# The FFN's normed rows turned on TensorE, three blocks' first products early, and the final norm's squares by halves, in an fp32 xLSTM/ConvFFN kernel

## The chip, the cores and the metric

The kernel runs on one core of a Trainium2 chip. The metric is the device time of one launch in microseconds. Three runs of the kernel before gave 1116.49, 1116.83 and 1116.87 us: a median of 1116.83. The trace is of one further execution of 1116.72 us, whose recorded span is 1115.0 us, so 1.72 us lie outside the span. Times below are us from the span's start.

The engines: TensorE (PE) multiplies, with its weight loads listed apart as PEld; VectorE (DVE) and ScalarE (ACT) work elementwise; GpSimd (POOL) does small things here; SyncE (SP) issues most DMAs. An engine's rows with a `q` at the end (SPq, ACTq) are its queue's own, such as DMA issues. Each engine runs its instructions strictly in its own order and waits on semaphores for the others.

## The reference

One layer on x of 1024 tokens x 1024, all fp32:

```python
x = x + mlstm_mixer(rmsnorm(x, norm_mix), ...)             # matrix memory in chunks of 64, then @ w_out
x = x + conv_ffn(rmsnorm(x, norm_ffn), w_up, conv_w, conv_b, w_down)
return rmsnorm(x, final_norm)

def rmsnorm(x, g):
    return x * lax.rsqrt(jnp.mean(x * x, axis=-1, keepdims=True) + EPS) * g
def conv_ffn(x, w_up, conv_w, conv_b, w_down):
    u = causal_dwconv(x @ w_up, conv_w, conv_b)            # 1024 -> 2 * 2816, width 3 along tokens
    gate, val = u[..., :2816], u[..., 2816:]
    return (jax.nn.silu(gate) * val) @ w_down              # 2816 -> 1024
```

The change touches what lies between the mixer's output projection and the up-projection, and the end.

## The kernel before

Every fp32 product is made of three matmuls in a rounded form (`mm3`, L119): each operand is split into a high part (`whi`, a cast on ScalarE) and the rest (`wlo`, a subtraction on VectorE), and low x high, high x high, high x low are summed in PSUM. "Matmul" below is one instruction with 128 x 128 weights and 512 columns.

Stages: norm and transposes of the input; projections; the mLSTM chunks up to about 345 us; the output projection by column halves, `out_proj(0, t)` and then `out_proj(1, t)` for the eight token tiles t (PSUM `pout`, added to the residual x on VectorE at L553); the FFN's norm; up-projection; down-projection; final norm.

**Seven products.** Up- and down-projection replace a 2 x 2 block product by seven block products (a Strassen-like scheme). For the up-projection tokens are halved (t < 4 and t >= 4) and the model dimension too. The seven right operands are b11, b21 (from the first tokens alone), b22 (second tokens alone), and the sums and differences t1 to t4 of quarters. Each is kept as a pair of high and low parts, `yc_...`; `put` (L615) writes one token tile of one of them: a cast of 128 x 512 on ScalarE (L620) and a subtraction on VectorE (L621). The rows of `yc_b...` are b11, b21, b22, those of `yc_t...` t1 to t4.

**Turning.** The operands need the normed rows `y` turned, with the model dimension on the partitions. `ffn_norm` (L623) takes the squares on ScalarE, the root on GpSimd (`rstd`), and makes both halves of y on VectorE (L628). For t < 7, y is written to DRAM block by block (`y_d`), read back as `flip_r`, and each half is turned within blocks of 32 by VectorE (`flip_halves`, L647, STREAM_TRANSPOSE at L652). For t = 7 eight TensorE transposes with an identity turn it in PSUM (`tp`, L659), and ScalarE copies both halves out (L660). `mix_a` (L662) then makes the differences and calls `put`.

**Up-projection.** 22 blocks of 128 hidden columns of gate and value, in the order 0, 11, 1, 12, 2, ... (HF = 11). A block needs its weights' pieces (`prep_first`: the gate's, `prep_rest`: value and sums, L703 to L727) and seven products of twelve matmuls, 84 in all, in `up` (L761). The results come together in `ug` and `uv` in SBUF: ScalarE copies a PSUM bank as a first term (L772, L775, L777, L787), VectorE adds others (L781, L783, L785). The products need six operands that are late, but b11 and b21 are complete early: `early` (L735) runs products 1 and 2 (`px`, `py`) of blocks 0 and 11 ahead of the turning of t = 7. Then come `pz`, the product with t1, and the others on the `px` and `pz` banks. PSUM has eight banks of 512 fp32 columns, here in groups: pa (two), pb (two), pc (four). `ug` and `uv` lie in the pool `late`, which is opened only after the pool `d2` with the turned rows is closed, so after the `put`s of t4 (L755 to L759).

**Down-projection.** Seven products again (924 matmuls, `pd`), the last of them, called 4, for the first column half: its blocks' weights come through the same `pieces` (L707, L708). It first finishes rows t = 0 to 3 beside it, then t = 4 to 7 at the very end. The final norm of row t: squares of both halves on ScalarE (L178, in `rms_scale`), root on GpSimd, the product of the first half with the gain (L896, GpSimd; VectorE for t = 7), its scaling on ScalarE (L902), the second half on VectorE (L904); the first half's output DMA is issued by ScalarE, the second's by SyncE (L903, L907), where the weight loads of the last blocks also queue.

The order of the instructions on each engine is set by a scheduler when the kernel is built, from the program's dependencies and the pools' buffers; `after` (L93) adds an order by hand in some places.

Of the kernel before, what the change touches and what calls it, by code (L numbers as in the profile page):

```python
# [43 lines left out]
def xlstm_convffn(  # L44
# [591 lines left out]
    def halves(t):  # L636
        lo_k = d2.tile([P, 516], F32, name="f0", tag="d2")[:, :512]
        if t < 4:
            if t % 2 == 0:
                b21[t // 2] = a4.tile([P, 2, 512], F32, name="b21", tag="a4")  # L640
            hi_k = b21[t // 2][:, t % 2]
        else:
            hi_k = d2.tile([P, 516], F32, name="f1", tag="d2")[:, :512]
        half_t[t] = [lo_k, hi_k]
        return half_t[t]
# [8 lines left out]
    def turn_halves(t, y):
        for a, dst in enumerate(halves(t)):
            ps = psa.tile([P, 512], F32, name="tp", tag="pc", bufs=4)
            yv = y[:, a * 512:(a + 1) * 512].rearrange("t (p k) -> t k p", k=4)
            for i in range(4):
                nc.tensor.transpose(ps[:, i * P:(i + 1) * P], yv[:, i], ident)  # L659
            nc.scalar.copy(dst, ps)  # L660

    def mix_a(t):  # L662
        f = half_t[t]
        if t < 4:
            if t == 0:
                combo("b11")
                combo("b21")
            put("b11", t, f[0])
            put("b21", t, f[1])
            return  # L670
# [24 lines left out]
    def prep_load(j):  # L695
        rg, rv = [rawp.tile([P, 1056], F32, name="raw", tag="raw") for _ in range(2)]
        for r, m in ((rg, j), (rv, NF + j)):
            v = r[:, :1024].rearrange("p (k c) -> p k c", c=P)
            for a in range(2):
                nc.sync.dma_start(out=v[:, a * NQ:(a + 1) * NQ], in_=w_up_v[:, a, :, m * P:(m + 1) * P])  # L700
        return rg[:, :1024], rv[:, :1024]
# [9 lines left out]
    def prep_first(j):  # L711
        rg, rv = prep_load(j)
        a11, a12 = pieces(rg)
        return rg, rv, a11, a12

    def prep_rest(rg, rv, a11, a12):
# [263 lines left out]
```

## Time and profile before

| what | value |
|---|---|
| median of three runs | 1116.83 us (1116.49 to 1116.87) |
| the profiled execution, its span | 1116.72 us, 1115.0 us |
| TensorE busy | 1071.9 us, 96% |
| VectorE, ScalarE, GpSimd busy | 775.5, 481.9, 77.4 us (70%, 43%, 7%) |
| TensorE's share of the chain that ended last | 77%; VectorE 11% |
| granted TensorE clock, mean over the span | 0.987 |
| bytes moved by DMA | 144.97 MB, 130 GB/s |
| last `pout` matmul, first `px`, first `pd`, last `pd` (starts) | 424.63, 424.87, 881.92, 1104.22 us |

The busy shares are of the whole span. The record of a busy matmul overlaps the next one, so a matmul's price is read from start to start. [...]

### The profile page before, as it was taken

Reading aid. Unit: us, or ns where it says so; the run is one execution under the profiler, and the core shown is the slowest. Engines: PE = TensorE matmul, PEld = TensorE weight load, DVE = VectorE, ACT = ScalarE, POOL = GpSimd, SP = SyncE. Lnnn points to the kernel's source line nnn. Section 1 sums busy time; section 2 is a strip of 40 time slices with the busy share of each in tenths; the row PEclk is TensorE's granted clock in tenths of the full one; section 3 lists DMA queues with packets and bytes.
Section 4 is the critical chain, followed back from the end, with each engine's and each line's share of the span. In section 5 each row is a group of like instructions: output and inputs, shape, how many; then the busy total and the mean of one; then the engine's idle time right before and its main releaser. Section 6 shows DMA issues by size and latency. Waiting matters only on the chain.

```text
span 1115.0 us, 13445 instructions
## 1 busy us (share of the span) xinstructions
PE 1071.9 (96%) x4918; PEld 876.6 (79%) x4918; DVE 775.5 (70%) x1146; ACT 481.9 (43%) x722; POOL 77.4 (7%) x155
## 2 busy tenths in 40 slices
PE   8999999999999995799999999999999999999985
PEld 7988888888887884588888888888888888888874
DVE  6733211488788469998978788787878778556564
ACT  6233111365453234454545454454545534433354
POOL 2000000123220011000000000000000000000042
PEclk9999999999999998799999999999999999999998
DMA  7722311024228475213331332233132895345653
GB/s 255 222 76 71 91 43 57 29 81 128 61 92 288 152 233 163 76 57 123 115 125 44 123 123 82 98 110 127 48 123 95 309 305 166 98 134 188 188 189 113
DMA packets 126091, 144.97 MB, mean 130 GB/s; under 512 B 8407, under 2 KB 87239, under 8 KB 126024
## 3 DMA queue, kind: packets, MB, share of 16 engines
q1 hardware_dynamic: 124872, 142.01, 39.5%
q10 hardware_dynamic: 1152, 2.10, 0.5%
q8 instruction: 38, 0.62, 0.2%
q14 instruction: 29, 0.24, 0.1%
HBM read 105.51 MB, written 38.57 MB: 129 GB/s over the span
## 4 chain that ended last, share of the span: by engine, by line
PE 77%; DVE 11%; DMA 4%; ACT 3%; issue 3%; POOL 2%; SPq 0%; POOLq 0%; ACTq 0%; DVEq 0%
PE px L122 7%; PE px L121 7%; PE px L120 7%; PE pd L121 5%; PE pd L120 5%; PE pd L122 5%; PE pz L122 4%; PE pz L121 4%; PE pz L120 3%; PE pqk L122 3%; PE pqk L121 3%; PE pqk L120 3%; PE pv L120 2%; PE pv L122 2%; PE pv L121 2%
## 5 line engine op out<-in xcount | busy, mean ns | idle before, releaser
L120 PE MATMUL pd<-wlo,whi 128*128 128x512 f32 x308 | 122.9, 399 | 4.2 <-DVE wlo L708 4.2
L707 ACT CAST whi<-raw 128x1024 fp32r<-128x1024 f32 x77 | 80.7, 1049 | 105.1 <-PE py L121 37.2
L121 PE MATMUL pd<-whi 128*128 128x512 f32 x308 | 122.9, 399 | 0.0
L122 PE MATMUL pd<-whi,wlo 128*128 128x512 f32 x308 | 121.1, 393 | 0.0
L120 PE MATMUL px<-yc_t,whi 128*128 128x512 f32 x264 | 105.2, 399 | 5.7 <-ACT ug L772 5.5
L708 DVE TENSOR_TENSOR wlo<-raw,whi 128x1024 fp32r<-128x1024 f32 x77 | 94.4, 1230 | 23.3 <-ACT whi L707 23.1
L122 PE MATMUL px<-yc_t,wlo 128*128 128x512 f32 x264 | 105.6, 400 | 0.0
L121 PE MATMUL px<-yc_t,whi 128*128 128x512 f32 x264 | 105.4, 399 | 0.0
L116 DVE TENSOR_TENSOR wlo<-raw,whi 128x1024 fp32r<-128x1024 f32 (+1 forms) x30 | 37.1, 1238 | 55.4 <-ACT whi L114 55.1
L120 PEld LDWEIGHTS pd<-wlo,whi 128*128 128x128 f32 x308 | 58.3, 189 | 20.9 <-DVE wlo L708 6.0
L707 ACT CAST whi<-s 128x1024 fp32r<-128x1024 f32 (+1 forms) x44 | 36.8, 836 | 77.2 <-PE px L121 39.4
L122 PEld LDWEIGHTS pd<-whi,wlo 128*128 128x128 f32 x308 | 58.1, 189 | 14.6
L114 ACT CAST whi<-raw 128x1024 fp32r<-128x1024 f32 (+1 forms) x30 | 31.3, 1051 | 87.1 <-PE pqk L121 37.4
L121 PEld LDWEIGHTS pd<-whi 128*128 128x128 f32 x308 | 58.1, 189 | 12.8
L120 PEld LDWEIGHTS px<-yc_t,whi 128*128 128x128 f32 x264 | 50.5, 191 | 18.7 <-ACT ug L772 5.9
L121 PEld LDWEIGHTS px<-yc_t,whi 128*128 128x128 f32 x264 | 50.2, 190 | 12.3
L122 PEld LDWEIGHTS px<-yc_t,wlo 128*128 128x128 f32 x264 | 50.2, 190 | 11.7
L796 DVE SCALAR_TENSOR_TENSOR acc<-ug,cw,acc 128x1024 f32<-128x1024 f32 x44 | 56.2, 1278 | 1.4 <-ACT acc L794 1.3
L796 DVE SCALAR_TENSOR_TENSOR acc<-uv,cw,acc 128x1024 f32<-128x1024 f32 x44 | 56.2, 1278 | 0.1
L881 ACT CAST whi<-raw 128x512 fp32r<-128x512 f32 x44 | 27.3, 621 | 59.4 <-PE pd L122 40.7
L882 DVE TENSOR_TENSOR wlo<-raw,whi 128x512 fp32r<-128x512 f32 x44 | 30.2, 687 | 27.7 <-ACT whi L881 27.6
L708 DVE TENSOR_TENSOR wlo<-s,whi 128x1024 fp32r<-128x1024 f32 (+1 forms) x44 | 41.9, 955 | 3.1 <-ACT whi L707 3.0
(265 smaller groups left out, 2680.6 us busy)
## 6 DMA issues: line engine op xcount, KB each, us to landing
raw<-in_l_ffn_w_up_dram SPq DMA_DIRECT2D x88, 256.0 KB, 3.4
raw<-h_d SPq DMA_DIRECT2D x77, 256.0 KB, 2.8
h_d<-acc SPq DMA_DIRECT2D x22, 512.0 KB, 3.4
raw<-in_l_ffn_w_down_dram SPq DMA_DIRECT2D x44, 256.0 KB, 3.5
h_d<-hx SPq DMA_DIRECT2D x11, 768.0 KB, 3.9
raw<-in_l_mlstm_w_in_dram SPq DMA_DIRECT2D x14, 512.0 KB, 5.0
keep<-in_l_ffn_w_down_dram SPq DMA_DIRECT2D x22, 256.0 KB, 4.6
raw<-in_l_mlstm_w_in_dram SPq DMA_DIRECT2D x16, 256.0 KB, 3.7
```

The source lines that it names most:

```text
L114: nc.scalar.copy(hi[:, :n], raw[:, :n])
L116: nc.vector.tensor_sub(lo[:, :n], raw[:, :n], hi[:, :n].bitcast(F32))
L120: nc.tensor.matmul(ps, a[0], b[1], start=first, stop=False, skip_group_check=chain)
L121: nc.tensor.matmul(ps, a[0], b[0], start=False, stop=False, skip_group_check=chain)
L122: return nc.tensor.matmul(ps, a[1], b[0], start=False, stop=last, skip_group_check=chain)
L707: nc.scalar.copy(hi[:, :n], src)
L708: nc.vector.tensor_sub(lo[:, :n], src, hi[:, :n].bitcast(F32))
L796: nc.vector.scalar_tensor_tensor(out=acc, in0=u[:, 2 - d:1026 - d], scalar=cw[:, tap, m:m + 1], in1=acc, op0=ALU.mult, op1=ALU.add)
L881: nc.scalar.copy(hi[:, sl], v)
L882: nc.vector.tensor_sub(lo[:, sl], v, hi[:, sl].bitcast(F32))
```

## The change

1. The row tiles t = 4, 5, 6 are turned like t = 7: by TensorE, with eight transposes each (`turned`). VectorE's differences and `put` read `tp` in PSUM directly; ScalarE copies one half of each row. `y_d` and `flip_halves` are left for t < 4. The pool for the read-backs has two buffers instead of three.
2. Three blocks' first products run early: 0, 11 and 1; block 1's in bank group pc. The gate's weights of these are loaded and split first; `prep_rest` loads the gate's weights again (512 KB more for each of the three).
3. `ug` of blocks below 11 has a pool of its own (`ugp`), opened earlier; `hx` goes from pool `sp` to `late`.
4. The final norm's square of a half is taken right after that half's last addition, by halves; the product with the gain is taken of the half that does not come last (GpSimd), and all output DMAs but the very last are issued by ScalarE.

```diff
-    flip_cm = tc.tile_pool(name="flip", side="right", bufs=3, reuse_waits="tile")
+    ugp_cm = tc.tile_pool(name="ugp", side="right", bufs=1, reuse_waits="tile")
+    flip_cm = tc.tile_pool(name="flip", side="right", bufs=2, reuse_waits="tile")
...
-            if t < NT - 1:
+            if t < 4:
                 flip_out(n, y[:, sl], y_d[t][:, :])
...
+    def turned(y, a, last):
+        ps = psa.tile([P, 512], F32, name="tp", tag="pa" if last else "pc", bufs=2 if last else 4)
+        yv = y[:, a * 512:(a + 1) * 512].rearrange("t (p k) -> t k p", k=4)
+        for i in range(4):
+            nc.tensor.transpose(ps[:, i * P:(i + 1) * P], yv[:, i], ident)
+        return ps
 
     def turn_halves(t, y):
         if t == 4:
             combo("b22")
             combo("t1")
+        b12, b22 = [turned(y, a, t == NT - 1) for a in range(2)]
         g = half_t[t - 4]
-        nc.vector.tensor_sub(g[0], f[0], g[0])
+        f = d2.tile([P, 516], F32, name="f0", tag="d2")[:, :512]
+        half_t[t] = [f]
+        nc.vector.tensor_sub(g[0], b12, g[0])
+        nc.scalar.copy(f, b12)
         put("t1", t, g[0])
-        nc.vector.tensor_sub(g[0], f[1], g[0])
-        nc.vector.tensor_sub(f[0], f[1], f[0])
+        put("b22", t, b22)
+        nc.vector.tensor_sub(g[0], b22, g[0])
+        nc.vector.tensor_sub(f, b22, f)
         nc.vector.tensor_sub(g[1], g[1], g[0])
-        put("b22", t, f[1])
...
-        if t >= 2:
+        if 2 <= t < 6:
             flip_halves(t - 2)
-            mix_a(t - 2)
-    flip_halves(NT - 2)
-    mix_a(NT - 2)
+        elif t >= 6:
+            turn_halves(t - 2, ys[t - 2])
+    turn_halves(NT - 2, ys[NT - 2])
...
-    for j in (0, HF):
-        first[j] = prep_first(j)
-    bank = {j: early(first[j]) for j in first}
-
+    for j, tag, bufs in ((0, "pb", 2), (HF, "pb", 2), (1, "pc", 4)):
+        first[j] = pieces(prep_load(j))
+        bank[j] = early(first[j], tag, bufs)
     turn_halves(NT - 1, ys[NT - 1])
-    mix_a(NT - 1)
-    ready = {0: prep_rest(*first[0])}
+    ready = {0: prep_rest(0, first.pop(0))}
...
-        ug = late.tile([P, 1028], F32, name="ug", tag="ug", bufs=2)
+        ug = (late if j >= HF else ugp).tile([P, 1028], F32, name="ug")
...
-        hx = sp.tile([P, 3, 512], F32, name="hx")
+        hx = late.tile([P, 3, 512], F32, name="hx")
...
+    def final_sq(t, n):
+        junk = const.tile([P, 512], BF16, name="junk", tag="junk")
+        nc.scalar.activation(junk, x1v(t, n), AF.Square, scale=1.0 / 32.0, accum_out=fss[:, t, n:n + 1])
+
+    def final_a(t):
         y = a4.tile([P, D], F32, name="yo", tag="a4")
-        eng = nc.vector if t == NT - 1 else nc.gpsimd
-        eng.tensor_tensor(y[:, :512], xv[0], g_fin[:, :512], op=ALU.mult)
-        fin[t] = (y, rms_scale(xv, "rstdf"))
+        n = 1 if t >= 4 else 0
+        nc.gpsimd.tensor_tensor(y[:, n * 512:(n + 1) * 512], x1v(t, n), g_fin[:, n * 512:(n + 1) * 512], op=ALU.mult)
+        r = small.tile([P, 1], F32, name="rstdf")
+        nc.gpsimd.tensor_scalar(
+            out=r, in0=fss[:, t, 0:1], scalar1=fss[:, t, 1:2], scalar2=EPS, op0=ALU.add, op1=ALU.add
+        )
+        nc.gpsimd.tensor_tensor(r, r, mhalf[:, :1], op=ALU.pow)
+        fin[t] = (y, r)
 
     def final_b(t):
...
-        nc.scalar.activation(y[:, :512], y[:, :512], AF.Copy, scale=r)
-        nc.scalar.dma_start(out=o[:, :512], in_=y[:, :512])
+        n = 1 if t >= 4 else 0
+        a, b = slice(n * 512, n * 512 + 512), slice((1 - n) * 512, (1 - n) * 512 + 512)
+        nc.scalar.activation(y[:, a], y[:, a], AF.Copy, scale=r)
...
-        nc.sync.dma_start(out=o[:, 512:], in_=y[:, 512:])
+        nc.scalar.dma_start(out=o[:, a], in_=y[:, a])
+        (nc.sync if t == NT - 1 else nc.scalar).dma_start(out=o[:, b], in_=y[:, b])
...
-            add = nc.vector.tensor_add(xv, xv, ps[i])
+            nc.vector.tensor_add(xv, xv, ps[i])
+            if q in (2, 3, 7, 4):
+                final_sq(t0 + i, n)
             if q == 4:
-                final_a(t0 + i, add)
-                if i:
-                    with after(add):
-                        final_b(t0 + i - 1)
-    final_b(NT - 1)
+                final_a(t0 + i)
+                final_b(t0 + i)
```

TensorE's order where the second early block meets the turning of t = 7, before (`px` and `py` are products 1 and 2 of a block, `y` the normed row):

```order
L121 MATMUL py<-yc_b_3609,whi 128x512
L122 MATMUL py<-yc_b_3609,wlo 128x512
L120 MATMUL px<-yc_b_3608,whi 128x512
L121 MATMUL px<-yc_b_3608,whi 128x512
L120 MATMUL py<-yc_b_3609,whi 128x512
L121 MATMUL py<-yc_b_3609,whi 128x512
L659 MATMUL tp<-ident,y_3854 128x128 x8
L122 MATMUL px<-yc_b_3608,wlo 128x512
```

and after, at the end of `out_proj(1, 7)`:

```order
L120 MATMUL pout<-wlo,hsT1h 128x512
L121 MATMUL pout<-whi,hsT1h 128x512
L122 MATMUL pout<-whi,hsT1l 128x512
L658 MATMUL tp<-ident,y_3746 128x128 x8
L658 MATMUL tp<-ident,y_3795 128x128 x8
L120 MATMUL px<-yc_b_3611,whi 128x512
L121 MATMUL px<-yc_b_3611,whi 128x512
```

The transposes of rows 5 and 6 now stand ahead of the first `px` (those of row 4 ahead of the last `pout`); those of row 7 stand behind the early products of three blocks, where they stood inside the second block's.

VectorE's order from the addition of t = 7 (L553, `x_3826`; after, `x_3829`) on, before:

```order
L553 TENSOR_TENSOR x_3826<-x_3826,pout 128x512
L652 STREAM_TRANSPOSE f_3868<-flip_r 128x4x128
L652 STREAM_TRANSPOSE f_3869<-flip_r 128x4x128
L628 SCALAR_TENSOR_TENSOR y_3854<-x_3405,rstd_3859,g_ffn 128x512
L628 SCALAR_TENSOR_TENSOR y_3854<-x_3826,rstd_3859,g_ffn 128x512
L675 TENSOR_TENSOR f_3658<-f_3868,f_3658 128x512
L621 TENSOR_TENSOR yc_b_3816<-f_3869,yc_b_3816 128x4x128
L678 TENSOR_TENSOR f_3868<-f_3869,f_3868 128x512
L621 TENSOR_TENSOR yc_t_3817<-f_3658,yc_t_3817 128x4x128
```

and after:

```order
L553 TENSOR_TENSOR x_3829<-x_3829,pout 128x512
L669 TENSOR_TENSOR f_3661<-tp,f_3661 128x512
L623 TENSOR_TENSOR yc_b_3807<-tp,yc_b_3807 128x4x128
L630 SCALAR_TENSOR_TENSOR y_3857<-x_3408,rstd_3862,g_ffn 128x512
L630 SCALAR_TENSOR_TENSOR y_3857<-x_3829,rstd_3862,g_ffn 128x512
L623 TENSOR_TENSOR yc_t_3808<-f_3661,yc_t_3808 128x4x128
L669 TENSOR_TENSOR f_3711<-tp,f_3711 128x512
L673 TENSOR_TENSOR f_3661<-tp,f_3661 128x512
L674 TENSOR_TENSOR f_3879<-tp,f_3879 128x512
```

The STREAM_TRANSPOSEs are gone from there, and the differences read `tp`. After the two halves of `y` of t = 7 (L630) come 26 rows up to the last part of t1 (`yc_t_3808`): 23 of 512 elements and three of 1024 (`wlo`), among them the first parts of t2 and t3.

ScalarE's order around the first block's gate copy (`ug<-px`), before; `yc_t_4032` is t4, `yc_t_3817` t1, `yc_t_4010` and `yc_t_4019` are t2 and t3:

```order
L620 CAST yc_t_4019<-f_3882 128x4x128
L620 CAST yc_t_4010<-f_3709 128x4x128
L620 CAST yc_t_3817<-f_3761 128x4x128
L620 CAST yc_t_4019<-f_3970 128x4x128
L620 CAST yc_t_4010<-f_3761 128x4x128
L707 CAST whi<-raw 128x1024
L707 CAST whi<-s_3992 128x1024
L707 CAST whi<-s_3993 128x512
L620 CAST yc_t_4032<-b_3605 128x4x128 x2
L620 CAST yc_t_4032<-b_3710 128x4x128 x2
L772 COPY ug<-px 128x512
L775 COPY uv<-pz 128x512
```

and after, where `yc_t_3808` is t1 and `yc_t_4056`, `yc_t_4065` are t2 and t3:

```order
L670 COPY f_3879<-tp 128x512
L622 CAST yc_t_3808<-f_3661 128x4x128
L761 COPY ug<-px 128x512
L670 COPY f_3899<-tp 128x512
L622 CAST yc_t_3808<-f_3711 128x4x128
L622 CAST yc_t_4056<-f_3661 128x4x128
L622 CAST yc_t_4065<-f_3879 128x4x128
L622 CAST yc_t_4056<-f_3711 128x4x128
L622 CAST yc_t_4065<-f_3899 128x4x128
```

The copy from `px` into `ug` stood behind all casts of t2, t3, t4 and the weights' casts; it now stands ahead of the casts of t2 and t3.

ScalarE's order at the end of the program, before (rows t = 5 to 7):

```order
L178 ACTIVATE junk,ss_8723<-xr_7041 128x512 x2
L902 ACTIVATE yo<-yo,rstdf 128x512
L178 ACTIVATE junk,ss_8749<-xr_7041 128x512
L903 DMA out_dram<-yo 128x512
L178 ACTIVATE junk,ss_8749<-xr_7041 128x512
L902 ACTIVATE yo<-yo,rstdf 128x512
L178 ACTIVATE junk,ss_8775<-xr_7041 128x512
L903 DMA out_dram<-yo 128x512
L178 ACTIVATE junk,ss_8775<-xr_7041 128x512
L902 ACTIVATE yo<-yo,rstdf 128x512
L903 DMA out_dram<-yo 128x512
```

and after (rows t = 5 to 7):

```order
L904 ACTIVATE yo<-yo,rstdf 128x512
L909 DMA out_dram<-yo 128x512
L908 DMA out_dram<-yo 128x512
L886 ACTIVATE junk,fss<-xr_7063 128x512 x2
L904 ACTIVATE yo<-yo,rstdf 128x512
L909 DMA out_dram<-yo 128x512
L908 DMA out_dram<-yo 128x512
L904 ACTIVATE yo<-yo,rstdf 128x512
L908 DMA out_dram<-yo 128x512
```

One square per row is left there instead of two, and ScalarE issues the second halves' output DMAs too (L909), except the last.

## Rows read from the trace of the kernel before

**Rows 1.** TensorE's waits: operation, releaser, us in total, times, longest.

```profile
PE px L122 <- DVE wlo L708: 7.8, 1, 7.8
PE px L120 <- ACT ug L772: 5.5, 1, 5.5
PE tp L659 <- DVE y L628: 5.0, 1, 5.0
PE pd L120 <- DVE wlo L708: 4.2, 3, 3.1
```

**Rows 2.** TensorE's timeline: start, us, operation, idle before it and releaser.

```profile
424.87 0.39 PE L120 MATMUL px<-yc_b,whi 128*128 128x512 f32 x1
...
436.52 1.89 PE L659 MATMUL tp<-ident,y 128*128 128x128 f32 x8 [5.01 <-DVE y L628]
446.17 0.80 PE L122 MATMUL px<-yc_b,wlo 128*128 128x512 f32 x1 [7.76 <-DVE wlo L708]
...
450.50 0.39 PE L122 MATMUL py<-yc_b,wlo 128*128 128x512 f32 x1
...
453.27 0.50 PE L120 MATMUL pz<-yc_t,whi 128*128 128x512 f32 x1 [0.28 <-ACT whi L707]
...
879.82 0.39 PE L120 MATMUL px<-yc_t,whi 128*128 128x512 f32 x1
...
881.92 0.40 PE L120 MATMUL pd<-wlo,whi 128*128 128x512 f32 x1
```

**Rows 3.** Windows: us; busy PE, PEld, DVE, ACT, POOL; PEclk; DMA share; GB/s.

```profile
20.00:24.00 4.00, 3.69 (x30) 3.49 (x29) 3.67 (x7) 2.79 (x9) 0.95 (x3) 1.00 0.23 68
440.00:450.00 10.00, 3.83 (x9) 3.07 (x10) 10.00 (x16) 5.18 (x9) 0.00 (x0) 0.50 0.00 1
450.00:460.00 10.00, 6.31 (x24) 4.16 (x23) 10.00 (x16) 3.44 (x5) 0.10 (x1) 0.98 0.35 104
```

**Rows 4.** VectorE's groups, 425 to 465 us: line, shapes, count, busy, mean ns, idle before.

```profile
L652 DVE STREAM_TRANSPOSE f<-flip_r 128x512 f32<-128x512 f32 x6 | 6.5, 1106 | 1.0 <-DMA flip_r<-y_d 1.0
...
L553 DVE TENSOR_TENSOR x<-x,pout 128x512 f32<-128x512 f32 x2 | 1.3, 660 | 0.0
```

**Rows 5.** TensorE's groups, 8 to 28 us: the transposes of the start.

```profile
L136 PE MATMUL tp<-ident,xt 128*128 128x128 f32 x32 | 5.9, 328 | 1.5 <-DVE xt L191 0.8 <-issue 0.4 <-PE pv L122 0.3
```

**Rows 6.** VectorE's timeline in the turning stage.

```profile
428.71 1.41 DVE L628 SCALAR_TENSOR_TENSOR y<-x,rstd,g_ffn 128x512 f32<-128x512 f32 x2 [0.85 <-POOL rstd L184]
...
433.05 0.68 DVE L553 TENSOR_TENSOR x<-x,pout 128x512 f32<-128x512 f32 x1
...
435.62 1.41 DVE L628 SCALAR_TENSOR_TENSOR y<-x,rstd,g_ffn 128x512 f32<-128x512 f32 x2
...
444.90 1.22 DVE L708 TENSOR_TENSOR wlo<-raw,whi 128x1024 fp32r<-128x1024 f32 x1
446.03 0.68 DVE L677 TENSOR_TENSOR f<-f,f 128x512 f32<-128x512 f32 x1
446.64 0.68 DVE L675 TENSOR_TENSOR f<-f,f 128x512 f32<-128x512 f32 x1
```

**Rows 7.** ScalarE's timeline: the casts of t4.

```profile
459.90 2.18 ACT L620 CAST yc_t<-b 128x512 fp32r<-128x512 f32 x4 [4.17 <-DVE yc_t L621]
```

**Rows 8.** SyncE's queue in the last product.

```profile
1079.15 4.05 SPq L907 DMA_DIRECT2D out_dram<-yo  x2
```

**Rows 9.** TensorE's timeline in the last product.

```profile
1084.04 0.50 PE L120 MATMUL pd<-wlo,whi 128*128 128x512 f32 x1 [3.07 <-DVE wlo L708]
```

**Rows 10.** Timeline of all engines at the end.

```profile
1104.22 0.40 PE L122 MATMUL pd<-whi,wlo 128*128 128x512 f32 x1
...
1105.16 0.67 DVE L940 TENSOR_TENSOR xr<-xr,pd 128x512 f32<-128x512 f32 x1
...
1108.82 0.30 POOL L181 TENSOR_SCALAR rstdf<-ss 128x1 f32<-128x1 f32 x1 [2.22 <-ACT junk L178]
...
1110.54 0.37 ACTq L903 DMA_DIRECT2D out_dram<-yo  x1
```

More of the change, by code (lines that the diff above doesn't have):

```diff
@@ L634, in ffn_norm @@
         return y
[L636 to L645, printed above, removed]
     def flip_halves(t):
@@ L650, in flip_halves @@
         rv = r.rearrange("p (b a i k) -> p a b k i", b=4, a=2, k=4)
-        for a, dst in enumerate(halves(t)):
+        if t % 2 == 0:
+            b21[t // 2] = a4.tile([P, 2, 512], F32, name="b21", tag="a4")
+        f = [d2.tile([P, 516], F32, name="f0", tag="d2")[:, :512], b21[t // 2][:, t % 2]]
+        for a, dst in enumerate(f):
             nc.vector.transpose(dst.rearrange("p (k j b) -> p b k j", k=4, b=4), rv[:, a])
-    def turn_halves(t, y):
[L655 to L670, printed above, removed]
+        half_t[t] = f
+        if t == 0:
+            combo("b11")
+            combo("b21")
+        put("b11", t, f[0])
+        put("b21", t, f[1])
+    def turned(y, a, last):
[4 more added lines that the diff above has]
+        return ps
+    def turn_halves(t, y):
         if t == 4:
@@ L693, in xlstm_convffn, with prep_load @@
     sp = sp_cm.__enter__()
[L695 to L701, printed above, removed]
+    def prep_load(m):
+        raw = rawp.tile([P, 1056], F32, name="raw", tag="raw")
+        v = raw[:, :1024].rearrange("p (k c) -> p k c", c=P)
+        for a in range(2):
+            nc.sync.dma_start(out=v[:, a * NQ:(a + 1) * NQ], in_=w_up_v[:, a, :, m * P:(m + 1) * P])
+        return raw[:, :1024]
     def pieces(src):
@@ L709, in pieces, with prep_rest @@
         return [(hi[:, i * 512:(i + 1) * 512], lo[:, i * 512:(i + 1) * 512]) for i in range(n // 512)]
[L711 to L716, printed above, removed]
+    def prep_rest(j, early_w=None):
+        rg, rv = prep_load(j), prep_load(NF + j)
+        a11, a12 = early_w or pieces(rg)
         s23 = sp.tile([P, 1024], F32, name="s23")
@@ L733, in product, with early @@
             mm3(ps, (w[0][:, ks], w[1][:, ks]), (yv[:, 0, k], yv[:, 1, k]), first and k == 0, k == NQ - 1, True)
-    def early(w):
-        x = psa.tile([P, 512], F32, name="px", tag="pb")
-        product(x, w[2], "b11", True)
+    def early(w, tag, bufs):
+        x = psa.tile([P, 512], F32, name="px", tag=tag, bufs=bufs)
+        product(x, w[0], "b11", True)
         y = psa.tile([P, 512], F32, name="py", tag="pc", bufs=4)
-        product(y, w[3], "b21", True)
+        product(y, w[1], "b21", True)
         return x, y
-    first = {}
-    for j in (0, HF):
-        first[j] = prep_first(j)
-    bank = {j: early(first[j]) for j in first}
+    first, bank = {}, {}
+    for j, tag, bufs in ((0, "pb", 2), (HF, "pb", 2), (1, "pc", 4)):
+        first[j] = pieces(prep_load(j))
+        bank[j] = early(first[j], tag, bufs)
     turn_halves(NT - 1, ys[NT - 1])
-    mix_a(NT - 1)
-    ready = {0: prep_rest(*first[0])}
-    for name, src in (("t2", 0), ("t3", 1)):
+    ready = {0: prep_rest(0, first.pop(0))}
+    for name, src in (("t2", 0), ("t3", 4)):
         combo(name)
         for t in range(4):
-            put(name, t, half_t[t + 4 * src][0])
+            put(name, t, half_t[t + src][0])
     d2_cm.__exit__(None, None, None)
@@ L821, in xlstm_convffn @@
             nj = order[i + 1]
-            ready[nj] = prep_rest(*(first.pop(nj) if nj in first else prep_first(nj)))
+            ready[nj] = prep_rest(nj, first.pop(nj, None))
         h = act(j, us)
@@ L890, in xlstm_convffn @@
     fin = {}
-    def final_a(t, add):
-        xv = [x1v(t, n) for n in range(2)]
-        y = a4.tile([P, D], F32, name="yo", tag="a4")
-        eng = nc.vector if t == NT - 1 else nc.gpsimd
-        eng.tensor_tensor(y[:, :512], xv[0], g_fin[:, :512], op=ALU.mult)
-        fin[t] = (y, rms_scale(xv, "rstdf"))
+    finp_cm = tc.tile_pool(name="finp", bufs=1, reuse_waits="tile")
+    finp = finp_cm.__enter__()
+    fss = finp.tile([P, NT, 2], F32, name="fss")
+    def final_sq(t, n):
+        junk = const.tile([P, 512], BF16, name="junk", tag="junk")
+        nc.scalar.activation(junk, x1v(t, n), AF.Square, scale=1.0 / 32.0, accum_out=fss[:, t, n:n + 1])
+    def final_a(t):
+        y = a4.tile([P, D], F32, name="yo", tag="a4")
+        n = 1 if t >= 4 else 0
[6 more added lines that the diff above has]
+        fin[t] = (y, r)
     def final_b(t):
@@ L933, in xlstm_convffn @@
             if q == 4 and 0 < k <= 4:
[L934 removed]
+                final_a(k - 1)
                 final_b(k - 1)
```

6 lines of the change are left out of this document (4 added, 2 removed).

## The prediction

> **What bounds the kernel now.** I read the busy table first: TensorE is busy for nearly the whole span, so what it loses is what can be won. The list of TensorE's waits [rows 1] says where: 18.3 us stand in three stops of 7.8, 5.5 and 5.0 us, each behind VectorE or ScalarE, and 4.2 us in the down-projection. TensorE's timeline places the three [rows 2]: all lie between the first `px` matmul (424.87) and the 463rd microsecond, where the normed rows are turned and mixed into the operands b22, t1, t2, t3, t4. The windows [rows 3] show who is full there: VectorE, 10.00 of 10 us twice, with TensorE's granted clock at 0.50 in the first of them. So the stretch is VectorE's. The up-projection behind it runs one matmul in (881.92 - 879.82)/9 = 0.2333 us [rows 2].
>
> Account of before, from first `px` to first `pd`: 457.05 us for 22 blocks x 84 = 1848 matmuls, which need 431.1. [...]
>
> **The turning (t = 4 to 7).** Removed: write-out and read-back of t = 4, 5, 6, with their six STREAM_TRANSPOSEs on VectorE (6.5 us busy, of which 0.1 each overlaps [rows 4]: 6 us) and the waits for `flip_r`. Added: 24 transposes on TensorE. In the one stretch with many, a transpose takes 328 ns in the mean, but overlapping [rows 5], with 30 matmul records in 4 us at clock 1.00 [rows 3], 0.13 each. I take 0.12: 2.8 us. Bounds: 24 x 0.06 = 1.4 (a quarter of a matmul's columns) and 24 x 0.24 = 5.7 (eight in 1.89 us at half clock [rows 2]). The subtractions now read PSUM. The nearest rows are the adds that read `pout`, 660 ns [rows 4]; an operation of that size from SBUF starts 0.61 after the last (446.03, 446.64 [rows 6]) and takes as long. I take no difference; bounds 1.2 us either way, for some twenty such operations.
>
> [...]
>
> Now the path, row by row of VectorE's new order. Before, the halves of `y` of t=6 start at 428.71 [rows 6]; their add no longer stands behind a STREAM_TRANSPOSE that waits for a transfer, worth up to 2 us; I take 1.4, so 427.3. Those two halves take 1.33, five operations of 512 3.0, one `wlo` of 1024 1.13 (444.90 to 446.03), so the add of t=7 starts at 432.8. From that add to `y` 2.57 us went by before (433.05 to 435.62: squares and root), so `y` of t=7 starts at 435.3, hardly earlier than now. From there to the last part of t1 stand 23 operations of 512 and three of 1024, 13.8 + 3.4 = 17.2. So t1 is whole at 435.3 + 1.33 + 17.2 + 0.1 = 453.9, and the first `pz` starts then, about where it starts now (453.27).
>
> TensorE comes there earlier. The second half of the transposes of t=6 wants a PSUM slot that VectorE frees four operations after `y` of t=6, at 431.1. `px` starts near 431.6, 6.7 later than before; but then 72 matmuls of three blocks run, 16.8 us, with about 1 of waiting on ScalarE's copies and 0.9 for the transposes of t=7. TensorE is done at 450.3 and waits 3.6 for t1. The stops of 5.0 and 7.8 us are gone, one of 3.6 takes their place, and at `pz` 24 more matmuls are done.
>
> **The third early block and the gate buffer.** From `pz` on, 1848 - 72 = 1776 matmuls are left instead of 1800: 414.3 us. The 5.5 us behind `ug` were an order on ScalarE: the copy that frees the block's bank stood behind four casts of t4, which waited 4.17 for VectorE [rows 7], because `ug` lay in a pool that opens after them. Now the copy stands far ahead of them. Late next are the last parts of t2 and t3, five operations of VectorE behind t1 (456.9, with TensorE there at 456.7), and the copies between the block's products: 0 to 0.8, I take 0.4. The clock: behind the stops of 5.0 and 7.8 us TensorE ran at half clock, so I charge one such stretch to the 3.6, at the 2.0 of before. First `pd`: 453.9 + 414.3 + 0.4 + 2.0 = 870.6, against 881.92: -11.3. The three added loads of 512 KB lie where the DMA engines idle (share 0.00 [rows 3]); without that cover each would hold SP and a buffer for some microseconds, ahead of weights that come due 10 us later. `hx` in another pool and the flip pool with two buffers I cost at nothing: two still let one transfer run while the other is turned; bound 1 us, if the first out-projection waits for a third.
>
> **The down-projection.** From 881.92 to 1104.22 [rows 2, 10] 923 steps need 215.4 and took 222.3: 6.9 lost. The largest part is one stop of 3.07 us with a fall of the clock behind it [rows 9]: SyncE's queue stood 4.05 us on two output DMAs that waited for ScalarE and VectorE, with the next weight loads behind them [rows 8]. After, these DMAs go to ScalarE's queue, and the squares of t = 0 to 3 are done earlier. But ScalarE's queue holds the weight casts, and each output DMA waits there for VectorE's half. I expect a stop of about that length again, and only the small ones gone: -0.8. Bounds: -5.7 (all but a little gone) and +2.
>
> **The end.** The last matmul is done at 1104.6; its add starts at 1105.16, behind VectorE's output half of the row before; then ScalarE squares both halves, the root starts at 1108.82, the last DMA issue at 1110.54 [rows 10], and the span ends at 1115.0. After, one half is squared beforehand, and the product with the gain is taken of the other half. Add at 1104.7, 0.7; one square 0.8; from root to issue 1.7 as now, so 1108.0, and 0.4 for what ScalarE's queue still has of t=6: 1108.4, -2.1; I take -1.9.
>
> **Sum:** -11.3 - 0.8 - 1.9 = -14.0 from the profiled execution's 1116.72 (span 1115.0; the median of the runs is 0.1 above it): 1102.7 us.
>
> **Rivals.** *The clock stays low* from the waits before `px` into the early products: 16 transposes at 0.24 instead of 0.12 and ten matmuls, 1.9 + 2.0 = 3.9 us; the wait at `pz` takes up only the first 0.5, since VectorE turns to the transposes of t=7 at 450.8. +3.4: 1106.1. For it: eight transposes behind a stop ran at half clock [rows 2]. Against: transposes among other matmuls ran at 1.00 [rows 3].
> [...] They stood alone only once, behind a 5.0 us stop, so the trace does not decide it.
>
> *VectorE stays the wall past `pz`*: the parts of t2, t3 and t4 are late too, a stop of 3.5 us comes at the second or third product, with another fall of the clock: +5.5, 1108.2. For it: VectorE is full to 460 [rows 3]. Against: six STREAM_TRANSPOSEs less stand ahead.
>
> *The last product runs free*, since SyncE no longer holds the weight loads: -4 more, 1098.7.
>
> *The change does little*: TensorE's early work only moves its wait to `pz`, and the transposes cost what VectorE sheds. The end's 1.9 then stands against 2.8: 1115 to 1117. Against it: 24 matmuls moved into idle time are 5.6 us by count alone.
>
> *Slower: banks.* Three held blocks keep six of the eight PSUM banks, and in blocks 0, 11 and 1 no second product is left to run while ScalarE copies the first, so each turns twice on one bank: six turns. From 2.3 us a turn, with copies behind casts on ScalarE as in the 5.5 us stop, the 14.0 are spent. At 3 us and one more fall of the clock: 1102.7 + 18 + 2 = 1122.7. Against it: before, two such blocks show that one stop.
>
> **Chances.** Forecast 0.60, clock 0.15, VectorE the wall 0.12, free product 0.05, little 0.04, slower 0.04. The forecast's own range is 1099 to 1106; with clock, wall and free product it is 1097.0 to 1108.5. About 0.2%, 2.2 us, can be told from no change: faster 0.93, same 0.03, slower 0.04.
>
> **What would show it.** Right: no wait over 1.5 us at the second early block; one of 3 to 4 at the first `pz`, behind VectorE; none behind `ug`; first `pd` between 869 and 872; last DMA issue about 4 us after the last matmul; one stop of 2 to 3.5 in the last product. Wrong: granted clock 0.5 at the first `px`, a second stop over 2 us before 470, waits on `ug` or `uv` in the first three blocks, or a first `pd` after 876.

## The result, and the profile after

Four runs of the changed kernel gave 1101.11 to 1106.35 us, median 1103.72, against 1116.76 (1116.49 to 1116.87) before: ratio 0.9884, 95% interval 0.986 to 0.9907. Four later runs (e12) gave 1104.32 to 1105.36, median 1105.25: ratio 0.9897, 0.9884 to 0.9911. The forecast of 1102.7 with 1097.0 to 1108.5 holds it. The profiled execution took 1104.03 us, 12.7 less than that of before, its span is 1102.1.

One correction of the text on the change: for t < 4 the half that GpSimd multiplies is the one that comes last (product 2 after product 3), not the earlier one.

TensorE's waits, for [rows 1] (operation, releaser, us in total, times, longest):

```profile
PE pd L120 <- DVE wlo L702: 5.4, 1, 5.4
PE pz L120 <- DVE yc_t L623: 2.8, 1, 2.8
PE tp L658 <- DVE f L674: 2.3, 1, 2.3
```

The stops of 7.8, 5.5 and 5.0 us are gone. Instead there are 1.0 and 2.3 before the two halves of the transposes of t = 6, 2.8 at `pz`, and one of 5.4 in the down-projection, where 4.2 stood in three. TensorE's timeline, for [rows 2, 9]:

```profile
428.78 0.72 PE L658 MATMUL tp<-ident,y 128*128 128x128 f32 x4 [1.05 <-DVE y L630]
431.84 1.10 PE L658 MATMUL tp<-ident,y 128*128 128x128 f32 x4 [2.34 <-DVE f L674]
432.59 0.77 PE L120 MATMUL px<-yc_b,whi 128*128 128x512 f32 x1
433.17 0.63 PE L121 MATMUL px<-yc_b,whi 128*128 128x512 f32 x1
...
451.44 1.12 PE L658 MATMUL tp<-ident,y 128*128 128x128 f32 x8
455.35 0.47 PE L120 MATMUL pz<-yc_t,whi 128*128 128x512 f32 x1 [2.79 <-DVE yc_t L623]
...
869.75 0.40 PE L120 MATMUL pd<-wlo,whi 128*128 128x512 f32 x1
...
1071.50 0.79 PE L120 MATMUL pd<-wlo,whi 128*128 128x512 f32 x1 [5.44 <-DVE wlo L702]
...
1092.56 0.40 PE L122 MATMUL pd<-whi,wlo 128*128 128x512 f32 x1
```

`px` starts at half clock (granted clock 0.50 from 432 to 437, one matmul each 0.43 us until 437.0, 2.0 lost), three blocks run through, the transposes of t = 7 follow at 451.44, `pz` at 455.35, and from there to the first `pd` 414.40 us pass, which is what 1776 matmuls need at the forecast's 0.2333 us (414.3). Behind the stop of 5.44 nine matmuls run 0.43 apart, 1.8 us lost (window as in [rows 3]):

```profile
1071.50:1075.40 3.90, 3.90 (x9) 3.12 (x10) 3.85 (x3) 0.00 (x0) 1.08 (x1) 0.51 0.59 172
```

VectorE's timeline, for [rows 6]:

```profile
427.88 1.42 DVE L630 SCALAR_TENSOR_TENSOR y<-x,rstd,g_ffn 128x512 f32<-128x512 f32 x2 [1.29 <-POOL rstd L184]
...
433.35 0.68 DVE L553 TENSOR_TENSOR x<-x,pout 128x512 f32<-128x512 f32 x1
...
435.92 1.41 DVE L630 SCALAR_TENSOR_TENSOR y<-x,rstd,g_ffn 128x512 f32<-128x512 f32 x2 [0.69 <-POOL rstd L184]
...
437.85 0.68 DVE L669 TENSOR_TENSOR f<-tp,f 128x512 f32<-128x512 f32 x1
438.45 0.68 DVE L673 TENSOR_TENSOR f<-tp,f 128x512 f32<-128x512 f32 x1
...
452.11 0.69 DVE L669 TENSOR_TENSOR f<-tp,f 128x512 f32<-128x512 f32 x1 [0.56 <-PE tp L658]
```

`y` of t = 6, the add of t = 7 and its `y` stand 0.5 to 0.6 us behind the forecast. VectorE then waits only 0.56 for the transposes of t = 7: it has been full in between, and it releases `pz`.

In the last product VectorE and GpSimd run beside each other (both engines' timelines, each row in a window that holds it alone):

```profile
1053.75 1.30 POOL L891 TENSOR_TENSOR yo<-xr,g_fin 128x512 f32<-128x512 f32 x1 [216.35 <-DVE xr L942]
1054.21 0.69 DVE L942 TENSOR_TENSOR xr<-xr,pd 128x512 f32<-128x512 f32 x1
...
1057.34 1.29 POOL L891 TENSOR_TENSOR yo<-xr,g_fin 128x512 f32<-128x512 f32 x1
1057.40 1.78 DVE L905 SCALAR_TENSOR_TENSOR yo<-xr,rstdf,g_fin 128x512 f32<-128x512 f32 x1 [1.80 <-POOL rstdf L896]
...
1063.71 0.75 DVE L905 SCALAR_TENSOR_TENSOR yo<-xr,rstdf,g_fin 128x512 f32<-128x512 f32 x1 [0.77 <-POOL rstdf L896]
...
1065.82 1.75 DVE L905 SCALAR_TENSOR_TENSOR yo<-xr,rstdf,g_fin 128x512 f32<-128x512 f32 x1 [0.76 <-POOL rstdf L896]
...
1067.49 1.75 DVE L863 TENSOR_TENSOR raw<-raw,tw 128x512 f32<-128x512 f32 x1
1068.65 1.71 POOL L891 TENSOR_TENSOR yo<-xr,g_fin 128x512 f32<-128x512 f32 x1
1069.16 2.28 DVE L702 TENSOR_TENSOR wlo<-raw,whi 128x1024 fp32r<-128x1024 f32 x1
...
1071.37 2.29 DVE L702 TENSOR_TENSOR wlo<-raw,whi 128x1024 fp32r<-128x1024 f32 x1
1073.59 1.21 DVE L702 TENSOR_TENSOR wlo<-raw,whi 128x1024 fp32r<-128x1024 f32 x1
```

A product on GpSimd takes 1.29 us when it begins first, and the output half that starts just behind it takes 1.78; with no product beside it such a half takes 0.75 (at 1063.71). From 1065.76 on GpSimd has four products in a row, those of rows t = 4 to 7: they take 1.26, 1.71, 1.71 and 2.09. Beside them an output half takes 1.75, a subtraction of 512 takes 1.75 instead of 0.68, and two `wlo` take 2.28 and 2.29; the third, with GpSimd done, takes 1.21. An addition that reads `pd` in PSUM (1054.21) and the product beside it are not held up: 0.69, where one with no product beside it takes 0.68 (1093.10), and 1.30. And at the end, for [rows 10]:

```profile
1093.10 0.68 DVE L942 TENSOR_TENSOR xr<-xr,pd 128x512 f32<-128x512 f32 x1
...
1093.65 0.39 ACTq L908 DMA_DIRECT2D out_dram<-yo  x1
...
1094.09 0.63 ACT L886 ACTIVATE junk<-xr 128x512 bf16<-128x512 f32 x1 [0.82 <-DVE xr L942]
...
1094.84 0.63 ACT L886 ACTIVATE junk<-xr 128x512 bf16<-128x512 f32 x1
...
1095.94 0.86 POOL L893 TENSOR_SCALAR rstdf<-fss 128x1 f32<-128x1 f32 x1
...
1098.29 0.35 ACTq L908 DMA_DIRECT2D out_dram<-yo  x1
```

Both squares of the end (t = 6 and 7) begin late: that of t = 6 stands behind two output DMA issues of t = 5 in ScalarE's queue (0.34 and 0.39 us, from 1093.21 on), and that of t = 7 behind it.

### The profile page after: what moved, and what is told of

It reads as the page before. It is cut to its first block, busy times and chain, and to the rows that moved or that the text cites. A ratio compares the mean times of both kernels' runs of the same rounds, so it can differ in the third digit from the quotient of the medians.

```text
span 1102.1 us, 13483 instructions
## 1 busy us (share of the span) xinstructions
PE 1071.0 (97%) x4942; PEld 877.7 (80%) x4942; DVE 770.1 (70%) x1139; ACT 481.6 (44%) x724; POOL 80.5 (7%) x156
## 4 chain that ended last, share of the span: by engine, by line
PE 82%; DVE 8%; DMA 3%; ACT 3%; POOL 2%; issue 2%; ACTq 0%; SPq 0%; POOLq 0%; DVEq 0%
PE px L122 7%; PE px L121 7%; PE px L120 7%; PE pd L120 6%; PE pd L121 6%; PE pd L122 6%; PE pz L122 4%; PE pz L121 4%; PE pz L120 4%; PE pqk L122 3%; PE pqk L121 3%; PE pqk L120 3%; PE pv L120 3%; PE pv L122 2%; PE pv L121 2%; PE py L122 2%
```

## The experiments

Times are medians; ratios are against the kernel before on the same chip, with 95% intervals. The changed kernel stands at 0.9884 and 0.9897.

**e1: the end as before.**

```diff
-            if q in (2, 3, 7, 4):
-                final_sq(t0 + i, n)
...
+        fin[t] = (y, rms_scale(xv, "rstdf"))
...
+        nc.sync.dma_start(out=o[:, 512:], in_=y[:, 512:])
```

> The changed kernel with the end of the program as it was before (squares of both halves per row, second halves' outputs from SyncE); the turning, the early blocks and the gate buffer stay changed. Theory (nearly all of the gain lies between the first px and the first pd): first pd stays at 869.8; the last product loses 6.9 us instead of 7.4, the end takes 10.4 instead of 9.2 us: about 1104.4, between 1103 and 1106. Rival (the end is worth the 2.7 us of the forecast): 1106.4 or more.

1104.7 us (1104.4 to 1108.06), 0.9897 [0.9884, 0.991]: the changed kernel's own value. First `pd` 869.66; the down-projection takes 222.7 from first to last matmul, as with the change (222.8); the end from the last matmul's start 10.2 us against 9.5. So the new end brings 0.7 us in the traces and nothing that the runs can tell. The theory holds.

**e2: t = 4 to 6 turned by VectorE.**

```diff
-            if t < 4:
+            if t < NT - 1:
                 flip_out(n, y[:, sl], y_d[t][:, :])
...
-            turn_halves(t - 2, ys[t - 2])
+            flip_late(t - 2)
```

> The changed kernel with rows t = 4, 5, 6 turned as before, by a write to DRAM, a read back and six STREAM_TRANSPOSEs on VectorE; the rest stays changed. Theory (VectorE's row of work sets the start of pz): six more operations of 1.0 us and their waits put the first pz from 455.4 to 461 or later, with a stop of 8 us or more before it and the clock low behind it: 1109 to 1113. Rival (the 24 transposes and their waits on TensorE cost what VectorE sheds): within 1.5 of 1103.7.

1108.1 us (1106.46 to 1111.47), 0.9919 [0.9906, 0.9931]. `pz` starts at 462.0 and the first `pd` at 876.98, but the long stop stands elsewhere, since the scheduler put the transposes of t = 7 and the third block otherwise. The read-backs have two buffers here, where the kernel before had three. The trace is of the longest of the six executions, 1111.47.

```profile
440.77 1.79 PE L658 MATMUL tp<-ident,y 128*128 128x128 f32 x8 [2.72 <-DVE y L630]
450.53 0.80 PE L122 MATMUL px<-yc_b,wlo 128*128 128x512 f32 x1 [7.97 <-DVE wlo L721]
...
462.00 0.40 PE L120 MATMUL pz<-yc_t,whi 128*128 128x512 f32 x1
```

Between the two forecasts in time, and with no wait at `pz` itself: TensorE comes there late, after a stop of 8 us that VectorE releases with a weight piece. So VectorE's work sets the time, as the theory has it, but at another place.

**e3: two early blocks.**

```diff
-    for j, tag, bufs in ((0, "pb", 2), (HF, "pb", 2), (1, "pc", 4)):
+    for j, tag, bufs in ((0, "pb", 2), (HF, "pb", 2)):
```

> The changed kernel with two blocks' first products early (0 and 11) instead of three. Theory (pz is set by VectorE, so 24 matmuls taken from in front of it leave TensorE idle there): the stop at pz grows from 2.8 to 8 us, first pd 5.6 us later, with the clock low behind the stop 7.6: 1109 to 1112. Rival (later operands are late anyway and the third block only moves the wait): 1103 to 1105.5.

1109.41 us (1107.17 to 1110.77), 0.9927 [0.9915, 0.9938]: in the theory's range, but not by its mechanism. There is no stop of 8 us at `pz`; the wait came out in pieces:

```profile
PE tp L658 <- ACT junk L178: 3.2, 1, 3.2
PE tp L658 <- DVE f L674: 2.2, 1, 2.2
PE pz L120 <- ACT uv L764: 2.0, 1, 2.0
```

First `pd` 872.60, 2.9 later than with the change, in an execution of 1107.17, the shortest of the five. The third block is worth 3 us in the traces and 3.4 to 4.8 by the ratios; why the runs show more stays open.

**e4: `ug` back in the late pool.**

```diff
-        ug = (late if j >= HF else ugp).tile([P, 1028], F32, name="ug")
+        ug = late.tile([P, 1028], F32, name="ug", tag="ug", bufs=2)
```

> The changed kernel with ug back in the pool that opens after the parts of t4. Theory (the copy of px into ug then stands behind four casts of t4 on ScalarE, which end at 461.0): the first product with t2 starts at about 461.6 instead of 458.3: +3.3, and +2 if the clock falls behind it: 1106.5 to 1109.5. Rival (that product is held by the last part of t2 on VectorE anyway): within 1 of 1103.7.

1109.73 us (1108.97 to 1111.25), 0.9931 [0.9919, 0.9943]: 0.2 above the theory's range. The stop is at the product that the theory named and as long (3.16 us at the product with t2), and the first `pd` 873.17, 3.4 later:

```profile
459.52 0.79 PE L120 MATMUL px<-yc_t,whi 128*128 128x512 f32 x1 [3.16 <-ACT ug L761]
```

**e5: the final rows t < 4 spread.** The same operations, begun three blocks later and queued behind weight pieces.

```diff
-            if q == 4 and 0 < k <= 4:
-                final_a(k - 1)
-                final_b(k - 1)
+            if q == 4 and 4 <= k <= 7:
+                final_a(k - 4)
+                final_b(k - 4, marks)      # behind block k's cast and subtraction
```

> The changed kernel with the final rows t = 0 to 3 begun three blocks later in the last product, VectorE's and ScalarE's part of each put behind the weight pieces of blocks 4 to 7; same operations. Theory (the 5.4 us stop comes from four output halves in a clump ahead of the weight pieces in VectorE's order, each waiting for GpSimd's product and root, 2.6 us a row): the stop falls under 1.5 us and the clock stays up there: 1098 to 1100.5. Rival (the casts stand behind output DMAs on ScalarE, which stay there): stop of 3.5 or more, 1102 to 1105.

1102.1 us (1101.35 to 1103.08), 0.9865 [0.9849, 0.9882]. In time this is the rival's range, 2.1 to 3.6 us under the changed kernel by the ratios, whose intervals overlap in one of the two comparisons. Three stops of 0.3, 2.0 and 1.25 us instead of one of 5.4: none is as long as the rival's, so the clump was a part; but 3.5 us remain and a `wlo` beside GpSimd's product takes 2.2. Neither theory had that.

**e6: rows t < 4 on VectorE alone.**

```diff
+        if t >= 4:
             nc.gpsimd.tensor_tensor(y[:, n * 512:(n + 1) * 512], x1v(t, n), ...)
...
+            nc.vector.scalar_tensor_tensor(
+                out=y[:, a], in0=x1v(t, n), scalar=r, in1=g_fin[:, a], op0=ALU.mult, op1=ALU.mult
```

> The changed kernel with both halves of the final rows t = 0 to 3 scaled and multiplied by the gain on VectorE (one operation each), without GpSimd's product and ScalarE's scaling. Theory (VectorE waits for GpSimd in its clump): four operations of 0.7 more, but 4.2 us of waits and some 3 us of slowed operations less: stop of 1 to 3 us, 1100 to 1102.5. Rival (ScalarE's queue with its eight output DMAs is what holds the casts): stop of 4.5 or more, 1103 to 1105.

1101.66 us (1100.73 to 1102.26), 0.9863 [0.9848, 0.9878], stops of 3.0 us in three, the longest 1.6: VectorE does four operations more and TensorE waits less. All eight output DMAs still stand on ScalarE's queue. The theory holds. GpSimd's products of rows t = 4 to 7 are left.

**e7: e5, and outputs at the end from SyncE.**

```diff
+        (nc.scalar if t < 4 or t == NT - 1 else nc.sync).dma_start(out=o[:, a], in_=y[:, a])
+        (nc.scalar if t < 4 else nc.sync).dma_start(out=o[:, b], in_=y[:, b])
...
+                    final_b(t0 + i - 1, (sq, add))
```

> As the spread version, and the output DMAs of rows t = 4 to 7 issued by SyncE (the first half of t = 7 by ScalarE), with each row's square ahead of the row before's scaling on ScalarE. Theory (at the end ScalarE's queue holds the squares behind two DMA issues of 0.34 to 0.44 a row): the last DMA issue comes 1 us earlier, 4.7 instead of 5.7 after the start of the last matmul: 1097 to 1099.5. Rival (the chain of the last row's addition, square and root alone sets the end): as the spread version within 0.5.

1104.09 us (1099.86 to 1104.7), 0.9877 [0.9856, 0.9898]: a miss in time for the theory and the rival; the trace is of the longest of the four. The end is as expected and better (last DMA issue 3.8 us after the last matmul's start, 5.7 with the change), but the last product has stops of 3.6 and 1.2, where e5 has three shorter ones: GpSimd's late products, which wait for a buffer (2.29 and 2.38 us), fall on VectorE's last pieces (two `wlo` from 1079.50 on take 3.44 together).

**e8: 64 transposes in a row.** Added work that nobody reads.

```diff
+        if i == 12:
+            tps = psa.tile([P, 512], F32, name="tps", tag="pc", bufs=4)
+            for _ in range(16):
+                for c in range(4):
+                    nc.tensor.transpose(tps[:, c * P:(c + 1) * P], ident, ident)
```

> The changed kernel with 64 more TensorE transposes of a constant in one run, between two blocks in the middle of the up-projection; nobody reads them. Theory (transposes keep the clock up like other matmuls): 64 x 0.115 = 7.4 us more, granted clock 1.00 during and behind them. Rival (transposes do not count as busy for the clock): the clock falls within them, the later ones start 0.2 apart and some ten matmuls behind them 0.43 apart: 10 us or more.

One run, 1111.03 us. The windows (us; busy PE, PEld, DVE, ACT, POOL; PEclk; DMA share; GB/s) and TensorE's timeline:

```profile
674.10:676.10 2.00, 2.00 (x20) 1.97 (x19) 2.00 (x3) 1.97 (x3) 0.00 (x0) 1.00 0.00 0
...
678.10:680.10 2.00, 2.00 (x21) 2.00 (x19) 2.00 (x3) 0.69 (x1) 0.00 (x0) 1.00 0.00 0
...
682.10:684.10 2.00, 2.00 (x10) 1.63 (x9) 1.93 (x3) 0.00 (x0) 0.00 (x0) 1.00 1.07 380
```

```profile
674.12 7.15 PE L812 MATMUL tps<-ident 128*128 128x128 f32 x64
681.03 0.47 PE L120 MATMUL px<-yc_b,whi 128*128 128x512 f32 x1
```

6.91 us from the first to the next matmul, 0.108 each, with the clock at 1.00 in them and behind them. The theory holds, for a run that begins at full clock; whether transposes bring the clock back from half, it does not show.

**e9: no product on GpSimd.** As e7, with the product on VectorE in place, right after the square. The eight products then run between 995 and 1030 us, ahead of the last product, and not in it.

```diff
-        nc.gpsimd.tensor_tensor(y[:, n * 512:(n + 1) * 512], x1v(t, n), g_fin[:, n * 512:(n + 1) * 512], op=ALU.mult)
...
+            if q in (3, 7):
+                nc.vector.tensor_mul(xv, xv, g_fin[:, n * 512:(n + 1) * 512])
```

> As the second spread version (e7), but the product with the gain is taken of the half finished earlier, by VectorE in place right after its square; GpSimd has only the roots left. Theory (GpSimd's product and VectorE's 1024-element subtraction slow each other: 2.2 us for a wlo beside a product against 1.23 alone): no wlo over 1.5 us in the last product, stops under 1 us in all, last product 5 us shorter than the changed kernel's: 1098 to 1099.5. Rival (the amount of VectorE's and ScalarE's work there holds the weights): stops of 2.5 us or more stay, 1100.5 to 1103.

1098.47 us (1097.74 to 1100.03), 0.9839 [0.9826, 0.9853]: the best version, 5 to 7 us under the changed kernel, and under e7 with intervals that do not overlap. First to last `pd` take 218.4 us instead of 222.8; stops of 2.3 in two remain, more than the theory's 1. VectorE's groups in the last product (line, shapes, count, busy, mean ns, idle before), with the change:

```profile
L702 DVE TENSOR_TENSOR wlo<-raw,whi 128x1024 fp32r<-128x1024 f32 x7 | 10.5, 1524 | 1.2 <-ACT whi L701 1.2
L905 DVE SCALAR_TENSOR_TENSOR yo<-xr,rstdf,g_fin 128x512 f32<-128x512 f32 x4 | 6.1, 1514 | 4.2 <-POOL rstdf L896 4.2
```

and in e9:

```profile
L703 DVE TENSOR_TENSOR wlo<-raw,whi 128x1024 fp32r<-128x1024 f32 x8 | 9.7, 1219 | 0.0
...
L906 DVE SCALAR_TENSOR_TENSOR yo<-xr,rstdf,g_fin 128x512 f32<-128x512 f32 x4 | 3.0, 745 | 0.0
```

The mean `wlo` falls from 1524 to 1219 ns, the output half from 1514 to 745, and its 4.2 us of waiting for the root are gone.

**e10: block 0's first product ahead of the transposes of t = 6.**

```diff
+    px0 = psa.tile([P, 512], F32, name="px", tag="pb", bufs=2)
+    product(px0, first[0][0], "b11", True)
     turn_halves(NT - 2, ys[NT - 2])
```

> The changed kernel with block 0's first product ahead of the transposes of t = 6, so that TensorE's waits of 1.0 and 2.3 us there are filled. Theory (the start of pz is VectorE's; the fall of the clock at the first px is nearly hidden): clock 1.00 at px, the transposes of t = 7 some 3 us earlier, VectorE's wait of 0.56 for them gone, pz 0.6 us earlier and nothing more, the stop at pz 5 us instead of 2.8 and the clock low behind it: 1103 to 1105. Rival (waits and low clock before pz are paid in full): 1099.5 to 1101.5.

1104.77 us (1103.74 to 1108.41), 0.9899 [0.9883, 0.9914]: as the theory has it in time. `px` starts at 427.13 at full clock, but the wait only moved: 2.8 us before `py`, for ScalarE's copy of a turned half, and the fall of the clock with it (granted 1.00 from 430 to 435, 0.66 from 435 to 440). So of the 5.5 us that `px` begins earlier 0.8 are left at the transposes of t = 7 (450.61 for 451.44). `pz` starts at 454.52, still 2.79 behind VectorE and not the 5 that the theory had.

```profile
427.13 0.48 PE L120 MATMUL px<-yc_b,whi 128*128 128x512 f32 x1
...
435.01 0.50 PE L120 MATMUL py<-yc_b,whi 128*128 128x512 f32 x1 [2.80 <-ACT f L670]
...
454.52 0.47 PE L120 MATMUL pz<-yc_t,whi 128*128 128x512 f32 x1 [2.79 <-DVE yc_t L623]
```

**e11: e9 and e10 together.**

> The two edits above together. Theory: they add: between 1097.5 and 1101, not below the no-product version by more than 1. Rival: 1096 or less.

1098.87 us (1098.56 to 1099.46), 0.9842 [0.9829, 0.9856]: e10 adds nothing to e9 either.

**e12: the changed kernel again.**

> The changed kernel once more, beside the three above. Theory: its runs spread by some 5 us, because each stop over 3 us may or may not be followed by a stretch at half clock (2 us) and the 5.4 us stop hangs on two engines' order: 1101 to 1106, with the granted clock lower in the longer runs. Rival (the spread came from one chip): within 1 us of each other.

1105.25 us (1104.32 to 1105.36), 0.9897 [0.9884, 0.9911], within 1.04 us here, so the rival's line is nearer for these runs. Its trace has `pz` 1.2 us earlier than the first (454.18), but the same first `pd` (869.73), for behind `pz` the clock fell, which it did not in the first. The same window in the first trace and in e12:

```profile
455.00:460.00 5.00, 4.65 (x20) 3.62 (x21) 5.00 (x10) 2.38 (x5) 0.24 (x3) 1.00 0.02 3
...
455.00:460.00 5.00, 5.00 (x17) 3.96 (x16) 5.00 (x10) 3.54 (x7) 0.23 (x3) 0.67 0.01 5
```

## Why the forecast came out

Its steps, against the first profiled execution:

| step | forecast | measured |
|---|---|---|
| first `px` | 431.6 | 432.59 |
| first `pz`, TensorE's wait before it | 453.9, 3.6 | 455.35, 2.79 |
| `pz` to first `pd` | 416.7 | 414.40 |
| first `pd` against before | -11.3 | -12.17 |
| first to last `pd` against before | -0.8 | +0.5 |
| last matmul to the span's end | -1.9 | -1.2 |
| outside the span | 0 | +0.2 |
| sum | -14.0 | -12.7 |

The total is nearer than its parts. `pz` came 1.45 us late, and from it to the first `pd` 2.3 us less passed than forecast; that one makes up for the other is luck. Of the signs that the forecast named for being right, three hold (no wait at the second early block, none behind `ug`, a first `pd` between 869 and 872) and three do not (3 to 4 us at `pz`: 2.79; the last DMA issue about 4 us after the last matmul: 5.7; a stop of 2 to 3.5 in the last product: 5.4). Of its four signs of being wrong two came (the granted clock of 0.5 at the first `px`, and a second stop over 2 us before 470: 2.34 and 2.79), and of waits on `ug` or `uv` there is one of 0.24.

**The turning: right.** VectorE's order gave the start of `pz` to 1.5 us: 0.6 of that are there at `y` of t = 7, and 0.56 are the wait for its transposes. e2 shows it with more work on VectorE: the stop that moves `pz` to 462.0 is VectorE's. e10 tests the other side only in part, since its own wait took back most of what was moved ahead. Operations that read `tp` in PSUM start 0.60 apart (437.85, 438.45 in the trace after), as one that reads SBUF alone does (439.65 to 440.25), so no cost there.

**The clock: the rival happened, and cost less than its price.** The forecast charged one fall, behind the 3.6 us; in the first trace it came at `px` instead, behind waits of 1.0 and 2.3, and cost VectorE a wait of 0.56 us. The 2.0 that it charged is what the trace before shows from 446.17 to 450.50: ten matmuls in 4.33 us, where 2.33 are needed at 0.2333 each, at a granted clock of 0.52. Seven traces have the same order up to the first `pd`. In six of them (e1, e5, e6, e7, e9, e12) the clock fell at both places: behind `pz`, after waits of 2.9 to 3.2, eight or nine matmuls ran 0.43 apart, and from `pz` to the first `pd` 415.5 to 415.6 us passed instead of 414.4. So the charged fall is real in six of the seven, at 1.15 us and not 2.0; in the first trace it did not come (granted clock 1.00 from 455 to 460). That transposes let the clock fall, as the rival of e8 has it, is not borne out: e8 ran 64 of them at 1.00, and in e10, too, the fall came behind the wait of 2.80 and not behind the transposes.

**The gate buffer and the third block: right in sign.** Undone alone they cost 3.8 to 5.2 and 3.4 to 4.8 us by the ratios, where the forecast has 5.5 for the stop and 5.6 for 24 matmuls; the turning, 2.5 to 3.9. Undoing the turning (e2) or the gate buffer (e4) brings, beside its stop, a further stretch at half clock (matmuls 0.43 apart from 451.12 to 454.96 in e2 and from 460.11 to 465.23 in e4; with the change the granted clock is 1.00 from 450 to 455 and from 458 to 466); undoing the third block does not. No run undoes two of them, so whether they add up is not shown.

**The down-projection: the step that failed.** "I expect a stop of about that length again, and only the small ones gone: -0.8." The stop grew from 3.07 to 5.4 us, and the stage by 0.5. The forecast looked for the cause in the queues that issue DMAs. What the runs show: VectorE's four output halves stand in a clump ahead of the weight pieces and wait 4.2 us for GpSimd (e5 takes the clump apart, e6 takes GpSimd's products of t = 0 to 3 away, and the stops get shorter in both), and VectorE and GpSimd hold each other up (a `wlo` takes 2.28 instead of 1.21, a product 1.71 instead of 1.29; e9 takes all eight products away, leaves the DMAs of t = 0 to 3 on ScalarE, and the time falls). The change itself brought the four products of t = 4 to 7 there, by giving GpSimd the half that is finished early, and the forecast had no term for it. With the end as before (e1) GpSimd has these products only from 1085.37 on, and SyncE's queue stands 4.01 us on two output DMAs, as in [rows 8]; the stage takes 222.7 us there and 222.8 with the change. One hold-up was exchanged for another. Without the products beside them, the half at 1065.82, the subtraction and the first `wlo` would have ended near 1068.3 instead of 1071.44 (an estimate from the 0.67, 0.60 and 1.21 that they take alone): 3.1 of the 5.4 us. No run takes these four products alone away.

The rows after show how long they are held up: the half at 1057.40, which takes 0.75 with no product beside it, ended 0.55 us after the end of its product, and the `wlo` at 1069.16, 1.21 without one, ended 1.08 after the end of the product at 1068.65. What holds them up no run shows.

The trace of the kernel before had the sign of it, which I did not read: VectorE's output half took 1.77 us beside a product (GpSimd's row at 1071.62), and the root's first step took 0.30 beside nothing and 1.41 beside a `wlo` and a subtraction (VectorE's rows at 1073.38 and 1074.52).

```profile
1071.69 1.77 DVE L904 SCALAR_TENSOR_TENSOR yo<-xr,rstdf,g_fin 128x512 f32<-128x512 f32 x1 [2.23 <-POOL rstdf L184]
...
1073.88 1.41 POOL L181 TENSOR_SCALAR rstdf<-ss 128x1 f32<-128x1 f32 x1 [0.97 <-ACT junk L178]
...
1077.40 0.30 POOL L181 TENSOR_SCALAR rstdf<-ss 128x1 f32<-128x1 f32 x1 [1.47 <-ACT junk L178]
```

**The end: the mechanism right, the size too large.** From the last matmul to the last DMA issue the time fell from 6.3 to 5.7 us, 0.6 where the forecast took 1.9. One square less saved 0.8 us up to the root, but ScalarE's queue took back some of it: the squares of t = 6 and 7 wait behind output DMA issues. From the root of t = 7 to the issue 2.35 us passed instead of 1.7, with its first step of 0.86 beside VectorE's output half. The other 0.6 of the 1.2 lies behind the last issue (4.4 us before, 3.8 after), for which the forecast had no term. With the outputs on SyncE (e7, e9) the last issue comes 3.8 us after the last matmul's start instead of 5.7.
